# Gated delta net heads: key norms inside the last projection, and a chain that begins with the key and value transposes

## The chip, the cores and the metric

One Trainium2 chip, one core of it. The metric is the device time of one execution in microseconds (us): the median of several runs. Engines: TensorE (PE, with PEld for its weight loads), VectorE (DVE), ScalarE (ACT), GpSimd (POOL) and SyncE (SP), which issues DMAs.

## The reference

One layer of a hybrid decoder step in float32, for 2048 prompt tokens, 16 meta tokens ahead of them and 8 x 4 sample tokens; width 1024. Four retention heads and four gated delta net heads of 128 read one input projection; then come the output projection, a layer norm and a SwiGLU network, which the change does not touch. The part that matters, for one gated head in chunks of 128 tokens:

```python
gq = l2_norm(conv[..., :W]...) * (HEAD_DIM ** -0.5)
gk = l2_norm(conv[..., W:2 * W]...)
...
decay = exp(G_i - G_j), lower triangle;  kk = k @ k.T
lower = where(strict, kk * decay, 0.0) * beta[..., :, None]
sol = triangular_solve(eye(C) + lower, concat([v * beta, k * (beta * gam)]), unit_diagonal=True)
attn = (q @ k.T) * decay
def step(s, xs):
    u = wv - wk @ s
    o = qg @ s + at @ u
    s = cd * s + kt.T @ u
```

The q, k and v of the head go through a causal convolution of width 4 and silu first; beta is a sigmoid of the projection.

## The kernel before

The first half of the span is attention: four blocks of 512 tokens (the first also has a tile of 48 rows with the sample and meta tokens, its "side" chain). In a block the heads go in the order r0 g0 r1 g1 r2 g2 r3 g3 (r retention, g gated; the last block r0 g0 g1 r1 g2 g3 r2 r3). For each head `ret_proj` or `gdn_proj` issues the projection, dense matmuls of high and low parts (line L406), and the head's chain of small dependent steps (`ret_chain`, `gdn_chain` with `gdn_group`) is started when its projection is issued. So the front of head g0's chain is written between the projection matmuls of r1, and so on; the chains fill PE's stream, and PE's projection matmuls cover the chains.

How they mix is set in Python. A projection is a generator that yields the time of each matmul step. `advance(us)` counts that time down for each active chain, and lets a chain issue its next piece, up to its next `yield`, when its count is used up. Each `yield` of a chain names an entry of the table LAT, multiplied by a slack that `pace` works out as 0.9 x PROJ x (projections until the next gated head) / INVERSE: INVERSE is the sum of a gated chain's entries up to its scan, so that this part spreads over the projections at hand. The tile framework then turns the program order into priorities and sets each engine's order; what is quoted below is that compiled order. Each engine runs its own list in order.

A gated head, lines of the kernel before: `flip(0)` and `flip(1)` in `gdn_proj` transpose q and k into PSUM (tag pj, two buffers, which the projections use as well), take the sums of squares on ACT (L811), and copy the keys to SBUF as `kp` (L815). Behind the last projection come the inverse square roots (`rsqrt`, L266 to L278) and the factors gsk (L873, L874). `gdn_group` then makes, for four chunks at once, mg (L916), U1 matmuls (L919), the exponential E (L923, ACT), Es and E masked (L924, L925, POOL), scaled keys (L933, DVE), transposed values and vb (L936, L937), transposed keys and their copy kT (L941, L943), kk matmuls (L947), LT = kk * Es (L949, DVE), Z and U (L958, L959, DVE), and six masked copies of LT for the levels of the inverse, Lm (L961, POOL). The levels of the inverse follow (L965 to L1001), then the scan over the four chunks (L1020 to L1057), in which the state S (L1051, DVE) of one chunk is read by the next chunk's first matmul (L1033, L1034).

A retention head, lines shared by both kernels: each tile of 128 tokens is rotated by two DVE products out of PSUM (L569 into `qk`, L570 into `rotB`) and one POOL addition (L571). Its chain transposes qk (L628, PE) and scales the keys into `rkd` (L632, DVE). `rotB` has two buffers, `qk` five.

Layer norm of the next block is issued at fixed steps of r1, g1, r2 and g2 (LN_AT): L307 on DVE and two L309 on POOL per tile, among small steps.

Of the kernel before, what the change touches and what calls it, by code (L numbers as in the profile page):

```python
# [8 lines left out]
F32 = mybir.dt.float32  # L9
# [4 lines left out]
ALU = mybir.AluOpType  # L14
# [4 lines left out]
HD = 128  # L19
# [12 lines left out]
RMS_EPS = 1e-6  # L32
NBLK = 4
CPB = 4
LN_AT = [(x, i) for x in ("r1", "g1", "r2", "g2") for i in (18, 26)]
LAT = [1.0, 0.7, 0.7, 0.7, 2.0, 0.7, 0.5, 1.2, 1.8, 1.8, 1.0, 1.0, 1.7, 1.0, 0.6, 0.5, 0.5, 1.2]
PROJ = 25.0
INVERSE = 21.0
REST = 8.0
# [200 lines left out]
class Builder:  # L240
# [545 lines left out]
    def gdn_proj(self, b, h, G, out):  # L786
        nc, mp, cp = self.nc, self.mp, self.cvp
# [12 lines left out]
        kps = []  # L800

        def flip(a):

            for ts in sets:
# [7 lines left out]
                if a:  # L812
# [3 lines left out]
                    kps.append(kp)  # L816

        for piece in range(2):
            wh, wl = self.next_piece()
            for part in range(2):  # L820
# [9 lines left out]
                for (c0, n) in groups:  # L830
# [3 lines left out]
                    for i, us in enumerate(steps):  # L834
                        yield us
                        if i == 5 and which % 2 and c0 == groups[-1][0]:
                            flip(which // 2)
                    if which < 3:
# [9 lines left out]
                if which < 3:  # L848
# [21 lines left out]
                    cv.append(o)  # L870
        rn = self.rsqrt(sq.rearrange("p a b -> p (a b)"), 2 * nt, 128, self.sm, 1.0, 4.0 * RMS_EPS).rearrange("p (a b) -> p a b", a=2)
        sk = self.sm.tile([128, 2, nt], F32, tag="gsk", name="gsk")
        nc.vector.tensor_scalar(out=sk[:, 0], in0=rn[:, 0], scalar1=HD ** -0.5, scalar2=None, op0=ALU.mult)  # L873
        nc.vector.tensor_tensor(out=sk[:, 1], in0=rn[:, 1], in1=G["sb"][:, :, h], op=ALU.mult)  # L874
        out += [cv, zg, sk, kps]

# [19 lines left out]
    def gdn_group(self, b, h, cv, zg, sk, kp, G, mixd, ts, tiles):  # L896
# [16 lines left out]


        mg = big("mg")[:R, :, :R]
        nc.vector.tensor_tensor(out=mg, in0=bc(M1), in1=G["g"][:R, ts[0]:ts[0] + m, h].unsqueeze(2).broadcast_to([R, m, R]), op=ALU.mult)  # L916
        pe = wide()
        for i in range(m):
            nc.tensor.matmul(pe[:R, i, :R], lhsT=U1, rhs=mg[:, i, :], start=True, stop=True)  # L919
        yield LAT[6]  # L920
        E = big("E", 2)[:R, :, :R]
# [3 lines left out]
        nc.gpsimd.tensor_tensor(out=E, in0=E, in1=bc(M1), op=ALU.mult)  # L925


        kp = kp[:R]
        vb = big("vb", 2, n=128)[:R]
        lane = lambda a: a.unsqueeze(2).broadcast_to([R, m, 128])  # L930
        here = slice(ts[0], ts[0] + m)
        cq = sk[:R, 0, here]
        nc.vector.tensor_tensor(out=kp, in0=kp, in1=lane(sk[:R, 1, here]), op=ALU.mult)  # L933
        p = wide()[:R, :m, :]
        for i in range(m):
            nc.tensor.transpose(p[:, i, :], v[:, col(i):col(i) + R], self.ident)  # L936
        nc.vector.tensor_tensor(out=vb, in0=p, in1=lane(G["sv"][:R, here, h]), op=ALU.mult)  # L937
        yield LAT[7]
        pk = wide()
        for i in range(m):  # L940
            nc.tensor.transpose(pk[:, i, :R], kp[:, i, :], idn)  # L941
        kT = big("kT", 2)[:, :, :R]
        nc.scalar.copy(out=kT, in_=pk[:, 0:m, :R])  # L943
        yield LAT[8]
        pl = wide()
# [14 lines left out]
        for x in range(1, nl):  # L960
            nc.gpsimd.tensor_tensor(out=Lm[:, x - 1], in0=LT, in1=lvl(x), op=ALU.mult)  # L961
        yield LAT[9]
        pt = wide()[:R, :m, :R]
# [3 lines left out]
        for x in range(1, nl):  # L967
            yield LAT[10]
            py = wide()[:R, :m, :R]
# [3 lines left out]
            nc.vector.scalar_tensor_tensor(out=Z, in0=py, scalar=-1.0, in1=Ib, op0=ALU.mult, op1=ALU.add)  # L973
            yield LAT[11]
            pt = wide()[:R, :m, :R]
# [11 lines left out]
        nc.scalar.copy(out=V, in_=U)  # L987
        yield LAT[12]
        pe = wide()[:R, :m, :R]
# [5 lines left out]
        for it in range(2):  # L995
            yield LAT[13]
            pu = wide()[:R, :m, :R]
            for i in range(m):
                nc.tensor.matmul(pu[:, i, :], lhsT=Er[:, i, :], rhs=V[:, i, :], start=True, stop=True)
            V = big(f"V{it}", 1, F32 if it else F32R)[:R, :, :R]  # L1000
            nc.vector.tensor_tensor(out=V, in0=U, in1=pu, op=ALU.add)  # L1001
# [14 lines left out]
        for i in range(m):  # L1016
# [15 lines left out]
            else:  # L1032
                nc.tensor.matmul(pp[:, 0, :], lhsT=kT[:, i, :], rhs=S, start=True, stop=True)  # L1033
                nc.tensor.matmul(po[:, 1, :], lhsT=q[:, c0:c0 + R], rhs=S, start=True, stop=True)  # L1034
            yield LAT[14]
            nc.vector.scalar_tensor_tensor(out=r[:orow], in0=pp[:orow, 0, :], scalar=gc("ng", i, orow), in1=vb[:orow, i, :], op0=ALU.mult, op1=ALU.add)
# [5 lines left out]
            nc.scalar.copy(out=u, in_=pp[:R, 2, :])  # L1042
            yield LAT[15]
            if sp:
# [593 lines left out]
```

## Time and profile before

| | |
|---|---|
| median of 3 runs | 2992.69 us (2990.74 to 2993.83) |
| profiled execution | 2997.01 us, of which the span is 2995.2 us |
| mean granted TensorE clock | 0.982 |
| busy: PE, DVE, ACT, POOL | 96%, 65%, 33%, 26% |
| POOL, six Lm of all heads (L961) | 129.2 us |
| PE waiting for the scaled keys (L941 on L933) | 13.9 us, 7 times |

Rows of groups read: line, engine, operation, output<-inputs, partitions x elements and types, count, busy us, mean ns of one, and after the second bar the engine's idle time before them with what ended it. Rows of the timeline read: start, duration, then the same. A buffer's number is left out in the profile and stands behind its name in the orders below. The profile's times belong to the one profiled execution.

### The profile page before, as it was taken

To read this page: it belongs to the slowest core of one execution; us is meant where nothing else is said; L and a number is where in the kernel's file an instruction comes from. 1 tells how busy PE (TensorE), PEld (TensorE's weight loads), DVE (VectorE), ACT (ScalarE), POOL (GpSimd) and SP (SyncE) were. 2 spreads that over 40 slices of the span, in tenths; PEclk is the share of its full clock that TensorE was granted. 3 is DMA by queue.
4 is the path that set the end of the run, shared out by engine and by line. 5 is a ranking of instruction groups with operands and counts; after the bars stand their busy time and mean duration, and the time that the engine had idled before them with its cause. 6 is when DMAs were issued, how large, how long until landed. Compare 5 with 4: busy or idle time off the path is not lost.

```text
span 2995.2 us, 47489 instructions
## 1 busy us (share of the span) xinstructions
PE 2864.0 (96%) x17942; PEld 2554.5 (85%) x17942; DVE 1932.5 (65%) x4203; ACT 998.9 (33%) x2352; POOL 783.7 (26%) x761
## 2 busy tenths in 40 slices
PE   7999999999999999989988999999999999999997
PEld 6878888888888878877777999999999999988895
DVE  7777667766776676667766666667644444844456
ACT  2434334444444444433233333333211112321121
POOL 1312222221222122225543433433200101411111
PEclk8989999999999999999999999999999999999998
DMA  7544534444444333356658666667755555787762
GB/s 259 203 171 154 200 122 152 148 170 153 150 157 154 135 121 122 125 166 232 216 196 289 249 222 229 227 231 266 271 182 187 176 183 183 272 292 239 243 226 86
DMA packets 223093, 580.89 MB, mean 194 GB/s; under 512 B 27296, under 2 KB 62672, under 8 KB 206480
## 3 DMA queue, kind: packets, MB, share of 16 engines
q1 hardware_dynamic: 222864, 577.86, 55.5%
q8 instruction: 141, 2.31, 0.3%
q14 instruction: 88, 0.72, 0.1%
HBM read 409.48 MB, written 168.30 MB: 193 GB/s over the span
## 4 chain that ended last, share of the span: by engine, by line
PE 77%; DVE 13%; DMA 3%; ACT 3%; issue 3%; POOL 1%; SPq 1%; POOLq 0%; ACTq 0%; DVEq 0%
PE d L406 20%; PE pj L406 19%; PE Z L406 8%; PE X L406 8%; PE Y L406 8%; PE W L406 4%; ACT junk L811 1%; DVE cacc L860 1%; PE w L978 1%; PE w L971 1%; PE pj L712 1%; PE w L980 1%; PE rt L666 1%; DVE wl L356 1%; DMA fr<-gu 1%
## 5 line engine op out<-in xcount | busy, mean ns | idle before, releaser
L406 PE MATMUL pj<-wh,xT 128*128 128x256 f32 (+2 forms) x2176 | 460.6, 295 | 6.7 <-ACT wh L349 3.0
L406 PE MATMUL pj<-xT,wh 128*128 128x512 f32 (+1 forms) x1280 | 380.3, 381 | 1.8 <-ACT cpre L844 1.1
L406 PEld LDWEIGHTS pj<-wh,xT 128*128 128x128 f32 (+1 forms) x2176 | 354.5, 189 | 11.8 <-ACT wh L349 3.3
L1495 DVE TENSOR_TENSOR y<-y,d 128x512 f32<-128x512 f32 (+1 forms) x344 | 234.8, 683 | 172.6 <-PE d L406 172.4
L406 PE MATMUL pj<-wl,xT 128*128 128x256 f32 (+3 forms) x1088 | 311.1, 286 | 0.6 <-POOL wl L356 0.5
L406 PE MATMUL d<-dh,fh 128*128 128x512 f32 (+1 forms) x745 | 297.9, 400 | 13.5 <-ACT dh L349 7.0
L406 PE MATMUL d<-dh,fl 128*128 128x512 f32 (+1 forms) x745 | 295.3, 396 | 0.0
L406 PE MATMUL d<-dl,fh 128*128 128x512 f32 (+1 forms) x745 | 294.2, 395 | 0.5 <-DVE dl L356 0.5
L356 POOL TENSOR_TENSOR fl<-ta,fh 128x384 fp32r<-128x384 f32 (+1 forms) x65 | 63.2, 972 | 768.3 <-issue 542.4
L406 PEld LDWEIGHTS pj<-xT,wh 128*128 128x128 f32 x1280 | 212.3, 194 | 25.6 <-DVE S L714 3.4
L406 PE MATMUL pj<-xT,wl 128*128 128x512 f32 (+1 forms) x640 | 230.1, 360 | 0.0
L406 PEld LDWEIGHTS pj<-wl,xT 128*128 128x128 f32 (+1 forms) x1088 | 205.8, 189 | 1.4 <-POOL wl L356 0.8
L406 PEld LDWEIGHTS d<-dh,fl 128*128 128x128 f32 (+1 forms) x745 | 137.4, 184 | 38.8 <-issue 0.5
L406 PEld LDWEIGHTS d<-dh,fh 128*128 128x128 f32 (+1 forms) x745 | 137.5, 185 | 32.8 <-ACT dh L349 7.3
L406 PEld LDWEIGHTS d<-dl,fh 128*128 128x128 f32 (+1 forms) x745 | 137.5, 185 | 20.7 <-DVE dl L356 1.0
L406 PEld LDWEIGHTS pj<-xT,wl 128*128 128x128 f32 x640 | 122.9, 192 | 16.8 <-issue 0.8
L860 DVE SCALAR_TENSOR_TENSOR cacc<-cpre,cw,cacc 128x512 f32<-128x512 f32 (+1 forms) x144 | 115.8, 804 | 32.4 <-ACT cacc L858 30.9
L1394 DVE TENSOR_TENSOR u<-x,Y 128x384 f32<-128x384 f32 (+1 forms) x132 | 67.5, 511 | 100.7 <-PE Y L406 97.8
L961 POOL TENSOR_TENSOR Lm<-LT,lvl 128x512 f16<-128x512 f32 (+1 forms) x108 | 129.2, 1228 | 11.3 <-DVE LT L949 10.5
L349 ACT CAST fh<-ta 128x384 fp32r<-128x384 f32 (+1 forms) x66 | 31.8, 482 | 287.7 <-DVE ta L1402 287.7
L406 PE MATMUL X<-b,a11h 128*128 128x384 f32 (+1 forms) x528 | 125.5, 323 | 1.8 <-ACT a11h L349 1.8
L406 PE MATMUL X<-b,a12h 128*128 128x384 f32 (+1 forms) x528 | 126.1, 325 | 0.0
(389 smaller groups left out, 7164.1 us busy)
## 6 DMA issues: line engine op xcount, KB each, us to landing
wh<-parts SPq DMA_DIRECT2D x45, 1024.0 KB, 5.2
wl<-parts SPq DMA_DIRECT2D x45, 1024.0 KB, 6.7
fr<-dn SPq DMA_DIRECT2D x66, 512.0 KB, 5.4
fr<-gu SPq DMA_DIRECT2D x44, 512.0 KB, 4.7
s12h<-wd SPq DMA_DIRECT2D x44, 512.0 KB, 4.9
s12l<-wd SPq DMA_DIRECT2D x44, 512.0 KB, 5.6
s34h<-wd SPq DMA_DIRECT2D x44, 512.0 KB, 3.8
s34l<-wd SPq DMA_DIRECT2D x44, 512.0 KB, 4.8
```

The source lines that it names most:

```text
L349: i = nc.scalar.copy(out=h, in_=src)
L356: i = (nc.vector if el == "dve" else nc.gpsimd).tensor_tensor(out=l, in0=src, in1=h.bitcast(F32), op=ALU.subtract)
L406: self.nc.tensor.matmul(out, lhsT=a(k), rhs=b(k), start=first and k == 0 and i == 0, stop=last and k == kn - 1 and i == 2, skip_group_chec ...
L666: nc.tensor.matmul(po, lhsT=sc, rhs=v, start=True, stop=False)
L712: nc.tensor.matmul(p, lhsT=kt, rhs=ub[:, 4 * i:4 * i + 4, :].rearrange("p a e -> p (a e)"), start=True, stop=True)
L811: nc.scalar.activation(out=junk, in_=p[:, j, :], func=AF.Square, accum_out=sq[:, a, t:t + 1])
L860: nc.vector.scalar_tensor_tensor(out=ac, in0=pre[:, i:i + N], scalar=w(i), in1=ac, op0=ALU.mult, op1=ALU.add)
L961: nc.gpsimd.tensor_tensor(out=Lm[:, x - 1], in0=LT, in1=lvl(x), op=ALU.mult)
L971: nc.tensor.matmul(py[:, i, :], lhsT=Lm[:, x - 1, i, :], rhs=T[:, i, :], start=True, stop=True)
L978: nc.tensor.matmul(pt[:, i, :], lhsT=U[:, i, :], rhs=Z[:, i, :], start=True, stop=True)
L1394: add = lambda o, x, p: nc.vector.tensor_tensor(out=o, in0=x, in1=p, op=ALU.add)
L1495: nc.vector.tensor_tensor(out=ys, in0=ys, in1=p, op=ALU.add)
```

## The change

`norms()` now does the inverse square roots, the factors gsk and the scaling of `kp`, and it is called among the matmul steps of the last projection of the head (step 4 of its last group; in the first block step 1). The keys' transposes, sums of squares and copy, `flip(1)`, move ahead in that projection: from step 5 of its last group to step 1 of its first (in the first block step 3). The chain now begins with the transposes of keys (L931 after) and values (L943), goes on with the U1 matmuls (L948) and everything up to the six Lm (L970) in a second piece. Two yields of the chain are gone, and INVERSE goes from 21.0 to 19.4, the new sum. No instruction is added or taken away. The later entries of LAT keep their values under new numbers.

```diff
--- before.py
+++ after.py
@@ -33,9 +33,9 @@
 NBLK = 4
 CPB = 4
 LN_AT = [(x, i) for x in ("r1", "g1", "r2", "g2") for i in (18, 26)]
-LAT = [1.0, 0.7, 0.7, 0.7, 2.0, 0.7, 0.5, 1.2, 1.8, 1.8, 1.0, 1.0, 1.7, 1.0, 0.6, 0.5, 0.5, 1.2]
+LAT = [1.0, 0.7, 0.7, 0.7, 2.0, 0.7, 0.9, 2.8, 1.0, 1.0, 1.7, 1.0, 0.6, 0.5, 0.5, 1.2]
 PROJ = 25.0
-INVERSE = 21.0
+INVERSE = 19.4
 REST = 8.0
 LEVELS = (1, 2, 4, 8, 16, 32, 64)
 
@@ -815,6 +815,19 @@
                     nc.vector.tensor_copy(out=kp, in_=p[:, :m])
                     kps.append(kp)
 
+        def norms():
+
+            rn = self.rsqrt(sq.rearrange("p a b -> p (a b)"), 2 * nt, 128, self.sm, 1.0, 4.0 * RMS_EPS).rearrange("p (a b) -> p a b", a=2)
+            sk = self.sm.tile([128, 2, nt], F32, tag="gsk", name="gsk")
+            nc.vector.tensor_tensor(out=sk[:, 1], in0=rn[:, 1], in1=G["sb"][:, :, h], op=ALU.mult)
+            for kp, ts in zip(kps, sets):
+                r = tiles[ts[0]][0]
+                here = slice(ts[0], ts[0] + len(ts))
+                nc.vector.tensor_tensor(out=kp[:r], in0=kp[:r], in1=sk[:r, 1, here].unsqueeze(2).broadcast_to([r, len(ts), 128]), op=ALU.mult)
+            nc.vector.tensor_scalar(out=sk[:, 0], in0=rn[:, 0], scalar1=HD ** -0.5, scalar2=None, op0=ALU.mult)
+            sks.append(sk)
+
+        sks = []
         for piece in range(2):
             wh, wl = self.next_piece()
             for part in range(2):
@@ -833,8 +846,12 @@
                     steps = self.mm3g(p, lambda k: wh[:, k, o:o + 128], lambda k: wl[:, k, o:o + 128], lambda k: xh[:, k, c0:c0 + n], lambda k: xl[:, k, c0:c0 + n], 8, 1)
                     for i, us in enumerate(steps):
                         yield us
-                        if i == 5 and which % 2 and c0 == groups[-1][0]:
-                            flip(which // 2)
+                        if which == 1 and i == 5 and c0 == groups[-1][0]:
+                            flip(0)
+                        if which == 3 and c0 == 0 and i == (3 if b == 0 else 1):
+                            flip(1)
+                        if which == 3 and c0 == groups[-1][0] and i == (1 if b == 0 else 4):
+                            norms()
                     if which < 3:
                         if b == 0 and c0 == 0:
                             nc.scalar.copy(out=pre[:, :hs].rearrange("p (b t) -> p b t", t=7)[:, :, 3:7], in_=p[:, :NS].rearrange("p (b t) -> p b t", t=4))
@@ -868,11 +885,7 @@
                     else:
                         nc.vector.scalar_tensor_tensor(out=o[:, :T], in0=th, scalar=1.0, in1=ac, op0=ALU.add, op1=ALU.mult)
                     cv.append(o)
-        rn = self.rsqrt(sq.rearrange("p a b -> p (a b)"), 2 * nt, 128, self.sm, 1.0, 4.0 * RMS_EPS).rearrange("p (a b) -> p a b", a=2)
-        sk = self.sm.tile([128, 2, nt], F32, tag="gsk", name="gsk")
-        nc.vector.tensor_scalar(out=sk[:, 0], in0=rn[:, 0], scalar1=HD ** -0.5, scalar2=None, op0=ALU.mult)
-        nc.vector.tensor_tensor(out=sk[:, 1], in0=rn[:, 1], in1=G["sb"][:, :, h], op=ALU.mult)
-        out += [cv, zg, sk, kps]
+        out += [cv, zg, sks[0], kps]
 
     def gdn_chain(self, b, h, cvz, G, mixd):
 
@@ -912,36 +925,32 @@
         Ib, Ih, idn = bc(self.ident[:R, :R]), self.identh[:R, :R], self.ident[:R, :R]
 
 
+        kp = kp[:R]
+        pk = wide()
+        for i in range(m):
+            nc.tensor.transpose(pk[:, i, :R], kp[:, i, :], idn)
+        kT = big("kT", 2)[:, :, :R]
+        nc.scalar.copy(out=kT, in_=pk[:, 0:m, :R])
         mg = big("mg")[:R, :, :R]
         nc.vector.tensor_tensor(out=mg, in0=bc(M1), in1=G["g"][:R, ts[0]:ts[0] + m, h].unsqueeze(2).broadcast_to([R, m, R]), op=ALU.mult)
+
+        vb = big("vb", 2, n=128)[:R]
+        lane = lambda a: a.unsqueeze(2).broadcast_to([R, m, 128])
+        here = slice(ts[0], ts[0] + m)
+        cq = sk[:R, 0, here]
+        p = wide()[:R, :m, :]
+        for i in range(m):
+            nc.tensor.transpose(p[:, i, :], v[:, col(i):col(i) + R], self.ident)
+        nc.vector.tensor_tensor(out=vb, in0=p, in1=lane(G["sv"][:R, here, h]), op=ALU.mult)
+        yield LAT[6]
         pe = wide()
         for i in range(m):
             nc.tensor.matmul(pe[:R, i, :R], lhsT=U1, rhs=mg[:, i, :], start=True, stop=True)
-        yield LAT[6]
         E = big("E", 2)[:R, :, :R]
         Es = mg
         nc.scalar.activation(out=E, in_=pe[:R, 0:m, :R], func=AF.Exp)
         nc.gpsimd.tensor_tensor(out=Es, in0=E, in1=bc(ST), op=ALU.mult)
         nc.gpsimd.tensor_tensor(out=E, in0=E, in1=bc(M1), op=ALU.mult)
-
-
-        kp = kp[:R]
-        vb = big("vb", 2, n=128)[:R]
-        lane = lambda a: a.unsqueeze(2).broadcast_to([R, m, 128])
-        here = slice(ts[0], ts[0] + m)
-        cq = sk[:R, 0, here]
-        nc.vector.tensor_tensor(out=kp, in0=kp, in1=lane(sk[:R, 1, here]), op=ALU.mult)
-        p = wide()[:R, :m, :]
-        for i in range(m):
-            nc.tensor.transpose(p[:, i, :], v[:, col(i):col(i) + R], self.ident)
-        nc.vector.tensor_tensor(out=vb, in0=p, in1=lane(G["sv"][:R, here, h]), op=ALU.mult)
-        yield LAT[7]
-        pk = wide()
-        for i in range(m):
-            nc.tensor.transpose(pk[:, i, :R], kp[:, i, :], idn)
-        kT = big("kT", 2)[:, :, :R]
-        nc.scalar.copy(out=kT, in_=pk[:, 0:m, :R])
-        yield LAT[8]
         pl = wide()
         for i in range(m):
             nc.tensor.matmul(pl[:R, i, :R], lhsT=kT[:, i, :], rhs=kT[:, i, :], start=True, stop=True)
@@ -959,19 +968,19 @@
         for x in range(1, nl):
             nc.gpsimd.tensor_tensor(out=Lm[:, x - 1], in0=LT, in1=lvl(x), op=ALU.mult)
-        yield LAT[9]
+        yield LAT[7]
...
```

Line numbers from here on differ: LT is L958 after (L949 before), Lm L970 (L961), Z L967, U L968, r L1045, the state S L1060 (L1051), and the scan's first matmuls L1042 and L1043 (L1033, L1034).

What stands where on the engines, first on PE at the front of the chain of the second block's first gated head. `kp_7216` (before) and `kp_7179` (after) are its keys, `pj` rows the projection of the retention head that is issued meanwhile. Before:

```order
L1052 MATMUL w_7291<-u_7286,E_6386 128x128
L406 MATMUL pj_7340<-wh_7053,xT_5230 128x256
L406 MATMUL pj_7340<-wl_7054,xT_5230 128x256
L406 MATMUL pj_7340<-wh_7053,xT_5230 128x256 x2
L941 MATMUL w_7359<-ident_66,kp_7216 128x128 x4
L406 MATMUL pj_7340<-wl_7054,xT_5230 128x256
```

After:

```order
L406 MATMUL pj_7366<-wh_7053,xT_5236 128x256 x2
L406 MATMUL pj_7366<-wl_7054,xT_5236 128x256
L931 MATMUL w_7295<-ident_66,kp_7179 128x128 x4
L943 MATMUL w_7305<-ident_66,post_7140 128x128 x4
L948 MATMUL w_7333<-mg_7302,cb_271 128x128 x4
L956 MATMUL w_7342<-kT_7300 128x128 x4
L406 MATMUL pj_7366<-wh_7053,xT_5236 128x256 x2
```

The value transposes and the matmuls of mg, which stood some ten rows ahead of the key transposes, now stand behind them, and the kk matmuls directly after those.

On POOL at the same place; `qk_7336`, `qk_7388`, `qk_7441`, `qk_7486` are the four tiles of the retention head r1 (before), `qk_7362`, `qk_7407`, `qk_7441`, `qk_7492` the same four (after). Before:

```order
L309 TENSOR_TENSOR xa_7087<-xa_7087,xa_6604 128x512 x2
L924 TENSOR_TENSOR mg_7294<-E_7307,cb_271 128x512
L571 TENSOR_TENSOR qk_7336<-qk_7336,rotB_7335 128x256
L925 TENSOR_TENSOR E_7307<-E_7307,cb_271 128x512
L571 TENSOR_TENSOR qk_7388<-qk_7388,rotB_7387 128x256
L571 TENSOR_TENSOR qk_7441<-qk_7441,rotB_7440 128x256
L961 TENSOR_TENSOR Lm_7428<-LT_7426,lvl_273 128x512 x6
L571 TENSOR_TENSOR qk_7486<-qk_7486,rotB_7485 128x256
L309 TENSOR_TENSOR xa_7523<-xa_7523,xa_6604 128x512 x2
```

After:

```order
L309 TENSOR_TENSOR xa_7101<-xa_7101,xa_6611 128x512 x2
L571 TENSOR_TENSOR qk_7362<-qk_7362,rotB_7361 128x256
L952 TENSOR_TENSOR mg_7302<-E_7338,cb_271 128x512
L953 TENSOR_TENSOR E_7338<-E_7338,cb_271 128x512
L970 TENSOR_TENSOR Lm_7349<-LT_7347,lvl_273 128x512 x6
L571 TENSOR_TENSOR qk_7407<-qk_7407,rotB_7406 128x256
L571 TENSOR_TENSOR qk_7441<-qk_7441,rotB_7440 128x256
L571 TENSOR_TENSOR qk_7492<-qk_7492,rotB_7491 128x256
L309 TENSOR_TENSOR xa_7530<-xa_7530,xa_6611 128x512 x2
```

The additions of the second and third tile stood ahead of the six Lm, and now stand behind them.

On DVE at the same place, from the second tile's rotation on. Before:

```order
L569 TENSOR_TENSOR qk_7388<-pj_7340,rott_5247 128x256
L570 TENSOR_TENSOR rotB_7387<-pj_7340,rott_5247 128x256
L1036 SCALAR_TENSOR_TENSOR r_7378<-sc_7383,ng_5963,vb_6390 128x128
L632 TENSOR_SCALAR rkd_7776<-qk_7388,cb_271 128x128
L569 TENSOR_TENSOR qk_7441<-pj_7392,rott_5247 128x256
L570 TENSOR_TENSOR rotB_7440<-pj_7392,rott_5247 128x256
L949 TENSOR_TENSOR LT_7426<-w_7421,mg_7294 128x512
L958 TENSOR_TENSOR Z_7429<-LT_7426,lvl_273 128x512
L1051 SCALAR_TENSOR_TENSOR S_gdn0_298<-S_gdn0_298,eg_5957,sc_7383 128x128
L959 SCALAR_TENSOR_TENSOR U_7430<-Z_7429,ident_66 128x512
L1053 SCALAR_TENSOR_TENSOR O_7284<-qs_7381,eg_5957,w_7384 128x128
```

After:

```order
L944 TENSOR_TENSOR vb_7304<-w_7305,sv_5833 128x512
L958 TENSOR_TENSOR LT_7347<-w_7342,mg_7302 128x512
L569 TENSOR_TENSOR qk_7407<-pj_7366,rott_5253 128x256
L967 TENSOR_TENSOR Z_7350<-LT_7347,lvl_273 128x512
L570 TENSOR_TENSOR rotB_7406<-pj_7366,rott_5253 128x256
L968 SCALAR_TENSOR_TENSOR U_7351<-Z_7350,ident_66 128x512
L1045 SCALAR_TENSOR_TENSOR r_7397<-sc_7402,ng_5970,vb_6383 128x128
L632 TENSOR_SCALAR rkd_7776<-qk_7407,cb_271 128x128
L569 TENSOR_TENSOR qk_7441<-pj_7411,rott_5253 128x256
L570 TENSOR_TENSOR rotB_7440<-pj_7411,rott_5253 128x256
L1060 SCALAR_TENSOR_TENSOR S_gdn0_298<-S_gdn0_298,eg_5964,sc_7402 128x128
```

Of the second tile, L632 (`rkd`) stood ahead of LT, and now stands six rows behind it, followed by the third tile's rotation and by the state `S_gdn0`.

More of the change, by code (lines that the diff above doesn't have):

```diff
@@ L967, in gdn_group @@
         for x in range(1, nl):
-            yield LAT[10]
+            yield LAT[8]
             py = wide()[:R, :m, :R]
@@ L973, in gdn_group @@
             nc.vector.scalar_tensor_tensor(out=Z, in0=py, scalar=-1.0, in1=Ib, op0=ALU.mult, op1=ALU.add)
-            yield LAT[11]
+            yield LAT[9]
             pt = wide()[:R, :m, :R]
@@ L987, in gdn_group @@
         nc.scalar.copy(out=V, in_=U)
-        yield LAT[12]
+        yield LAT[10]
         pe = wide()[:R, :m, :R]
@@ L995, in gdn_group @@
         for it in range(2):
-            yield LAT[13]
+            yield LAT[11]
             pu = wide()[:R, :m, :R]
@@ L1034, in gdn_group @@
                 nc.tensor.matmul(po[:, 1, :], lhsT=q[:, c0:c0 + R], rhs=S, start=True, stop=True)
-            yield LAT[14]
+            yield LAT[12]
             nc.vector.scalar_tensor_tensor(out=r[:orow], in0=pp[:orow, 0, :], scalar=gc("ng", i, orow), in1=vb[:orow, i, :], op0=ALU.mult, op1=ALU.add)
@@ L1042, in gdn_group @@
             nc.scalar.copy(out=u, in_=pp[:R, 2, :])
-            yield LAT[15]
+            yield LAT[13]
             if sp:
@@ L1057, in gdn_group @@
             nc.scalar.activation(out=junk, in_=O[:orow, i, :], func=AF.Square, scale=cq[:orow, i:i + 1], accum_out=ss[:orow, i:i + 1])
-            yield LAT[16]
+            yield LAT[14]
         rs = self.rsqrt(ss[:orow], m, orow, self.sm, 1.0 / HD, RMS_EPS)
@@ L1062, in gdn_group @@
         nc.vector.tensor_tensor(out=O[:orow], in0=O[:orow], in1=rs.unsqueeze(2).broadcast_to([orow, m, 128]), op=ALU.mult)
-        yield LAT[17]
+        yield LAT[15]
         for i in range(m):
```

## Prediction

> **What bounds the kernel now.** I read the page first.
>
> ```profile
> span 2995.2 us, 47489 instructions
> PE 2864.0 (96%) x17942; PEld 2554.5 (85%) x17942; DVE 1932.5 (65%) x4203; ACT 998.9 (33%) x2352; POOL 783.7 (26%) x761
> PEclk8989999999999999999999999999999999999998
> ```
>
> TensorE is busy 96% of the span. A change that alters no instruction count can therefore only move the time in which PE waits, and the clock that it is granted. PE's waits by what ended them come second (total, times, longest, in us):
>
> ```profile
> PE w L941 <- DVE kp L933: 13.9, 7, 2.6
> PE w L919 <- DVE V L1001: 0.9, 4, 0.2
> PE pj L406 <- DVE kp L815: 0.7, 2, 0.4
> ```
>
> The key transposes L941 wait for the scaling of the keys, L933, and this is the largest wait at the front of a head's chain. The timeline of one such place, the second block's first gated head, shows why (start, duration, both in us):
>
> ```profile
> 568.69 1.28 POOL L924 TENSOR_TENSOR mg<-E,cb 128x512 f32<-128x512 f32 x1
> 568.94 1.05 DVE L277 SCALAR_TENSOR_TENSOR rqt<-rqt,rqa 128x8 f32<-128x8 f32 x1
> 571.09 1.26 POOL L925 TENSOR_TENSOR E<-E,cb 128x512 f32<-128x512 f32 x1
> 571.16 1.27 DVE L632 TENSOR_SCALAR rkd<-qk,cb 128x128 f32<-128x128 f32 x1
> 572.35 0.68 DVE L933 TENSOR_TENSOR kp<-kp,gsk 128x512 f32<-128x512 f32 x1
> 573.18 1.09 PE L941 MATMUL w<-ident,kp 128*128 128x128 f32 x4 [2.56 <-DVE kp L933]
> ```
>
> ```profile
> 934.96 1.09 PE L941 MATMUL w<-ident,kp 128*128 128x128 f32 x4 [2.57 <-DVE kp L933]
> ...
> 218.44 0.66 PE L941 MATMUL w<-ident,kp 128*128 128x128 f32 x4 [2.07 <-DVE kp L933]
> ```
>
> The first of these is the last of four alike (at 573, 646, 862 and 935 us); the other is the longest of the remaining three. DVE is late: its small steps of the norm wait in its queue, and L277 and L632 are drawn out to 1.05 and 1.27 us until the POOL multiplication beside them ends. Then come the windows around three such gaps (columns: the stretch, its length, PE, PEld, DVE, ACT, POOL busy, granted clock, DMA):
>
> ```profile
> 572.00:576.00 4.00, 2.82 (x14) 2.85 (x15) 1.75 (x5) 0.98 (x3) 0.35 (x1) 0.58 0.43 135
> 576.00:580.00 4.00, 4.00 (x36) 4.00 (x36) 1.70 (x6) 0.53 (x2) 0.73 (x1) 0.99 0.00 0
> ...
> 645.00:649.00 4.00, 2.69 (x19) 2.72 (x20) 2.90 (x8) 1.20 (x4) 0.72 (x2) 0.84 0.66 206
> 649.00:653.00 4.00, 4.00 (x28) 4.00 (x28) 0.31 (x2) 0.31 (x2) 0.49 (x1) 0.73 0.00 0
> 214.00:218.00 4.00, 2.12 (x16) 1.92 (x16) 3.95 (x15) 1.59 (x4) 0.72 (x1) 1.00 0.31 131
> 218.00:222.00 4.00, 3.56 (x29) 3.37 (x30) 3.87 (x10) 1.05 (x3) 0.74 (x1) 1.00 0.91 275
> ```
>
> A gap of 2.56 us costs more than itself: the clock behind it is 0.58 for 4 us, a loss of 0.42 x 4 = 1.7 us. At 645 to 653 it is (0.16 + 0.27) x 4 = 1.7 us. At 214 to 222, around the gap of 2.07 us, the clock stays 1.00. The row 576:580 also gives PE's pace at full clock: 36 records in 4.00 us, 0.111 us each.
>
> **What the change can gain.** The norms and the scaling move into the last projection, so that the transposes need not wait for them. At most this gains the 13.9 us, four clock losses of 1.7 us (6.8; the four of 2.56 or 2.57 us), and the small rows above (0.9 + 0.7): 22.3 us. It will not be all. In the four 2.5-us places the next block's layer norm runs on DVE and POOL at the same time, and the changed order on DVE still has the scaling (now L826) behind the elementwise step on E (0.68 in the row's form), L307 on 128x1024 (1.23), two small steps and one L570. Counted from the time at which E's matmuls were done before (566), E ends at 567 to 568, and the scaling at 569.7 to 570.8. PE has moved earlier too: 22 short matmuls (2.4 us) and two waits fewer stand before its transposes, which it reaches near 568.6 to 569.2. So about 0.5 to 2.2 us of wait stays in each of the four, with or without the 1.7 of clock: 2 to 16 us, and I take 8. The two waits fewer give the other steps 8% more spacing each, which I cost at nothing: PE has projection work between them. **Gain: 15 us, between 6 and 20.**
>
> **What the change can lose.** Here the order matters more than the edit. Before, POOL does the additions L571 of the following retention head's tiles between the chain's steps, and the six multiplications Lm come after the third. After, Es, E and the six Lm stand ahead of the second L571 (the orders are in the section on the change). And on DVE the reader of that second tile, L632 on qk_7407, moves to six rows behind LT. Each engine takes its instructions in order. So DVE has to wait at L632 until POOL has done Es, E, six Lm and one L571, all of which hang on this same chain. The durations (groups by form; the number before the bar is busy, then mean ns):
>
> ```profile
> L961 POOL TENSOR_TENSOR Lm<-LT,lvl 128x512 f16<-128x512 f32 x96 | 126.4, 1348 | 11.3 <-DVE LT L949 10.5
> L571 POOL TENSOR_TENSOR qk<-qk,rotB 128x256 f32<-128x256 f32 x64 | 48.3, 757 | 160.8 <-DVE rotB L570 141.6 <-DVE rqy L278 10.6 <-PE sc L1050 6.0
> L924 POOL TENSOR_TENSOR mg<-E,cb 128x512 f32<-128x512 f32 x16 | 20.7, 1296 | 113.4 <-ACT E L923 102.4 <-DVE rqt L276 11.0
> L925 POOL TENSOR_TENSOR E<-E,cb 128x512 f32<-128x512 f32 x16 | 20.4, 1272 | 0.6
> L923 ACT ACTIVATE E<-w 128x512 f32<-128x512 f32 x16 | 9.6, 597 | 16.0 <-PE w L919 16.0
> L569 DVE TENSOR_TENSOR qk<-pj,rott 128x256 f32<-128x256 f32 x64 | 26.7, 417 | 38.8 <-PE pj L406 38.6
> L959 DVE SCALAR_TENSOR_TENSOR U<-Z,ident 128x512 f16<-128x512 f16 x16 | 23.2, 1451 | 0.2
> L958 DVE TENSOR_TENSOR Z<-LT,lvl 128x512 f16<-128x512 f32 x16 | 11.7, 729 | 0.5
> L949 DVE TENSOR_TENSOR LT<-w,mg 128x512 f32<-128x512 f32 x16 | 11.0, 689 | 2.7 <-PE w L947 1.4
> L1051 DVE SCALAR_TENSOR_TENSOR S_gdn<-S_gdn,eg,sc 128x128 f32<-128x128 f32 x64 | 21.8, 341 | 22.3 <-PE sc L1050 22.0
> ```
>
> That such an addition really stands behind the six, and what they take together, is seen at 581 us of the timeline, where its operand from L570 was ready at 585.5 and it began at 589.0; there nothing on DVE needed it soon. The next row is what DVE waits for these additions now, in the whole run:
>
> ```profile
> 581.26 7.73 POOL L961 TENSOR_TENSOR Lm<-LT,lvl 128x512 f16<-128x512 f32 x6
> 585.10 0.41 DVE L570 TENSOR_TENSOR rotB<-pj,rott 128x256 f32<-128x256 f32 x1
> 588.96 0.77 POOL L571 TENSOR_TENSOR qk<-qk,rotB 128x256 f32<-128x256 f32 x1
> ...
> L961 POOL TENSOR_TENSOR Lm<-LT,lvl x108: 264/1164/1677, 119.3 to 1245.1; 128x512 f16<-128x512 f32 x96, 48x48 f16<-48x48 f32 x12
> ...
> DVE rkd L632 <- POOL qk L571: 10.6, 14, 2.0
> ```
>
> Take the head of the second block, and L as the end of the chain's first matmuls (L948 in the new code). Exp ends at L + 0.7, Es at L + 2.0, E at L + 3.3; the six Lm take 7.0 (six of the median 1.16) to 7.73, I take 7.4: L + 10.7. One L571: 11.4. L632, 0.28 undisturbed: 11.7. Behind it on DVE stand L569 and L570 of the third tile (0.8) and the state's update, 0.33: the state S is ready at L + 12.8. PE meanwhile: the kk matmuls (1 us), 29 short matmuls (3.2) and the load of the next one bring it near L + 4.6 to L1050, whose operand r stands on DVE behind LT, Z, two rotation steps and U: 2.0 + 0.7 + 0.4 + 0.7 + 0.4 + 1.4 + 0.35 = L + 5.95. It waits 1.4. Then 28 short matmuls, 3.1 us, and it stands at L1042 at L + 9.1, which reads S: it waits 3.7. Together 5.1 us, and the second wait is longer than the 2.56 that cost clock, so 1.7 on top: 6.8 us.
>
> This pattern, L632 six to twelve rows behind LT with its addition behind the six Lm, is in 14 of the 16 heads' orders; only two heads of the last block, followed by another gated head, are free of it. Counting the same rows in each: four heads as above, 4 x 6.8 = 27. Four heads where L632 is nine rows behind and PE's own rows last longer (waits 0.2 and 2.0, clock half the times, 0.8): 4 x 3.0 = 12. Two heads at a block's end, where the first tile's transposes L628 on PE and the splits of the next block's x also stand behind the addition (0.7 + 0.7 + 2.5 + 1.0, clock 1.7): 2 x 6.6 = 13. Four heads of the first block, where the small side chain's steps stand between: between the second and the first kind, 4 x 4.5 = 18. **Loss: 70 us.** Its lower end: if PE reaches S late, only the second kind everywhere, 14 x 2.2 = 31. Its upper end: 7.73 for Lm and 1.7 of clock for each of two waits, 14 x 7 = 98.
>
> **A rule beside it.** The pages bear on one term, the length of the six Lm. The Trainium skill ("SBUF — State Buffer", section "Who interferes with whom") says that DVE and GpSimd share one pair of ports as an exclusive lock, that a DVE instruction with two SBUF inputs contends with a GpSimd instruction reading SBUF, and that the loser blocks for the winner's whole instruction; the drawn-out L277 and, next to E, L632 agree. By it, a DVE that sits waiting leaves POOL alone, and the six would take the undisturbed 7.0 us rather than 7.4: the loss would be 14 x 0.4 = 6 us smaller, and the time 3042.
>
> **The sum.** +70 - 15 = +55 us against the profiled execution's 2997.0. That execution is 4.3 us above the median of the runs, 2992.7, and I set the sum on the median: 2993 + 55 = 3048 us.
>
> **Rivals.**
> First, the change does what it says and the additions cost nothing: faster. Place: L1042 in each head. It needs S by L + 9.1 instead of L + 12.8, so the six Lm would have to take 3.7 us in place of 7.4, 0.6 us each, or DVE's wait would have to fall where PE has other work of 4 us queued. The 1.16 of the median speaks against it. Time: 2993 - 15 = 2978, at best 2970.
> Second, the wait is there but smaller: PE is itself delayed by r and by its transposes, so that it comes to S later, and the clock stays up. The lower end, 31, less a gain of 15 to 20: 3004 to 3010. For it: gaps near 2 us cost no clock.
> Third, the wait is worse than summed: LT, which now follows Es closely, is late as well, and PE's short waits (0.2 to 1.4) add to the long one within one clock window. 98 - 10: 3080.
> Fourth, no change: gain and loss cancel, which takes a loss of 9 to 21 us, 1 us in each head.
>
> **How the numbers follow.** The summed case 0.62 (own range 3025 to 3068); smaller waits 0.16; worse waits 0.10; no net change 0.04; faster 0.08. A measurement of this kernel can hardly tell less than 0.2%, 6 us, from no change. Slower by more than that: 0.62 + 0.16 + 0.10 = 0.88; within it 0.04; faster 0.08. The range reaches from the second case's lower end to the third's value, 3003 to 3080; beyond it lie the faster case, no change, and a part of the worst.
>
> **What would show it.** In the changed kernel's waits, DVE L632 on POOL L571 should rise from 10.6 us, longest 2.0, to some 60 to 90 us, longest near 5 to 6. PE's waits on S at L1042, now absent among the large ones, should be the largest in attention, about 3.7 us each; the granted clock should show half-speed windows behind them. PE's wait for the keys' scaling should fall from 13.9 to about 5. If L632's wait stays near 10 us, the step on POOL's order is wrong, and the first rival holds. If PE waits at L1042 for under 1 us, DVE's wait lay beside other work. If Lm takes under 1 us each, its duration was the mistake.

## The result

The changed kernel takes 3048.0 us (median of 4 runs, 3046.1 to 3050.3); the kernel before took 2993.3 us beside it. The ratio is 1.0185, 95% interval 1.0173 to 1.0198: slower by 55 us. The forecast was 3048.

The profile's page of the changed kernel, and of its chain of waits the line by engine; behind them the same line of the kernel before:

```profile
span 3044.9 us, 47475 instructions
PE 2873.5 (94%) x17942; PEld 2567.2 (84%) x17942; DVE 1916.3 (63%) x4203; ACT 996.2 (33%) x2352; POOL 785.6 (26%) x761
PE 72%; DVE 11%; POOL 7%; issue 3%; DMA 3%; ACT 3%; SPq 1%; POOLq 0%; ACTq 0%; DVEq 0%
```

```profile
PE 77%; DVE 13%; DMA 3%; ACT 3%; issue 3%; POOL 1%; SPq 1%; POOLq 0%; ACTq 0%; DVEq 0%
```

No engine was given more work: each has as many instructions as before. POOL's busy time rose by 2 us, DVE's fell by 16, and PE's rose by 10, at a mean granted clock of 0.978 instead of 0.982. But POOL's part of the chain that ends last went from 1% to 7%. An engine that is busy a quarter of the time became one that others wait for. What PE waits for now (total, times, longest, in us), then the rows for r and S in the kernel before, and then the two rows of DVE that belong to it:

```profile
PE sc L1042 <- DVE S_gdn L1060: 20.6, 10, 3.5
...
PE sc L1050 <- DVE r L1045: 15.2, 13, 3.1
...
PE w L974 <- DVE U L968: 6.1, 3, 3.0
...
PE w L931 <- DVE kp L826: 3.2, 6, 0.7
```

```profile
PE sc L1041 <- DVE r L1036: 1.5, 1, 1.5
...
PE sc L1033 <- DVE S_gdn L1051: 0.6, 2, 0.3
```

```profile
DVE rkd L632 <- POOL qk L571: 55.4, 23, 5.9
...
DVE LT L958 <- POOL mg L952: 27.6, 12, 4.7
```

The change did what its words say: the key transposes' wait for the scaled keys fell from 13.9 to 3.2 us. Against that, DVE's wait for the additions rose from 10.6 to 55.4 us, and two waits of PE rose: on the state S, which DVE makes behind L632, from 0.6 to 20.6 us, and on r, which DVE makes ahead of L632 but now behind LT, Z and U, from 1.5 to 15.2 us. The place that the prediction worked through, in the timeline (start and duration in us; the brackets give the idle time before and what ended it):

```profile
584.83 1.27 POOL L952 TENSOR_TENSOR mg<-E,cb 128x512 f32<-128x512 f32 x1 [1.00 <-ACT E L951]
586.13 0.69 DVE L958 TENSOR_TENSOR LT<-w,mg 128x512 f32<-128x512 f32 x1 [1.38 <-POOL mg L952]
...
587.43 7.65 POOL L970 TENSOR_TENSOR Lm<-LT,lvl 128x512 f16<-128x512 f32 x6
...
589.90 0.49 PE L1050 MATMUL sc<-r,V 128*128 128x128 f32 x2 [1.51 <-DVE r L1045]
595.04 0.72 POOL L571 TENSOR_TENSOR qk<-qk,rotB 128x256 f32<-128x256 f32 x1
595.79 0.29 DVE L632 TENSOR_SCALAR rkd<-qk,cb 128x128 f32<-128x128 f32 x1 [5.95 <-POOL qk L571]
...
596.66 0.34 DVE L1060 SCALAR_TENSOR_TENSOR S_gdn<-S_gdn,eg,sc 128x128 f32<-128x128 f32 x1
...
597.05 0.69 PE L1042 MATMUL sc<-S_gdn,kT 128*128 128x128 f32 x2 [3.46 <-DVE S_gdn L1060]
```

The six Lm run from 587.4 to 595.0. The last operand of L571, from L570 on DVE, was ready at 588.4; L571 starts as the six end. DVE stands idle for 5.95 us at L632, with the state's update only three instructions behind it, and PE waits 1.51 us for r and 3.46 us for S. The windows around it (stretch, length, PE, PEld, DVE, ACT, POOL busy, granted clock, DMA):

```profile
590.00:594.00 4.00, 3.59 (x31) 3.34 (x31) 0.00 (x0) 0.27 (x1) 4.00 (x5) 1.00 0.00 0
594.00:598.00 4.00, 0.95 (x5) 0.95 (x6) 2.05 (x7) 0.65 (x3) 2.48 (x3) 0.90 0.00 0
598.00:602.00 4.00, 4.00 (x27) 3.99 (x27) 0.97 (x4) 0.75 (x3) 0.73 (x1) 0.67 0.39 111
```

In the first stretch DVE does nothing at all while POOL is busy throughout. The clock behind the wait is lowered for a while: (0.10 + 0.33) x 4 = 1.7 us more, the price that gaps of 2.56 us had before.

### The profile page after: what moved, and what is told of

It is laid out like the page before. It is cut to its first block, busy times and chain, and to the rows that moved or that the text cites. A ratio compares the mean times of both kernels' runs of the same rounds, so it can differ in the third digit from the quotient of the medians.

```text
span 3044.9 us, 47475 instructions
## 1 busy us (share of the span) xinstructions
PE 2873.5 (94%) x17942; PEld 2567.2 (84%) x17942; DVE 1916.3 (63%) x4203; ACT 996.2 (33%) x2352; POOL 785.6 (26%) x761
## 4 chain that ended last, share of the span: by engine, by line
PE 72%; DVE 11%; POOL 7%; issue 3%; DMA 3%; ACT 3%; SPq 1%; POOLq 0%; ACTq 0%; DVEq 0%
PE d L406 19%; PE pj L406 17%; PE X L406 8%; PE Y L406 8%; PE Z L406 8%; PE W L406 4%; POOL Lm L970 4%; DVE cacc L877 1%; POOL mg L952 1%; DVE rqt L272 1%; PE w L980 1%; PE pj L712 1%; PE w L987 1%; POOL E L953 1%; PE w L989 1%
## 5 line engine op out<-in xcount | busy, mean ns | idle before, releaser
L406 PEld LDWEIGHTS pj<-wh,xT 128*128 128x128 f32 (+1 forms) x2176 | 361.3, 193 | 13.8 <-ACT wh L349 4.2
L970 POOL TENSOR_TENSOR Lm<-LT,lvl 128x512 f16<-128x512 f32 (+1 forms) x108 | 130.4, 1238 | 0.2 <-DVE LT L958 0.2
L406 PE MATMUL W<-t,a22h 128*128 128x384 f32 (+1 forms) x528 | 126.3, 325 | 0.0
```

The costliest lines, as they stand in the source:

```text
L406: self.nc.tensor.matmul(out, lhsT=a(k), rhs=b(k), start=first and k == 0 and i == 0, stop=last and k == kn - 1 and i == 2, skip_group_chec ...
```

## The experiments

Theory 1: an addition L571 that DVE needs soon stands behind the six Lm in POOL's list; DVE waits in order, and PE with it. Theory 2: the front of the chain is too tight without its two yields, whatever POOL does. Theory 3: the norms and transposes cost, moved into the last projection. Each time is a median, each ratio against the kernel before in the same session.

**Half of Lm left out**, in the changed kernel (the later levels read the third copy again, so the inverse is not the true one and only the time counts):

```diff
-        for x in range(1, nl):
+        for x in range(1, min(nl, 4)):
             nc.gpsimd.tensor_tensor(out=Lm[:, x - 1], in0=LT, in1=lvl(x), op=ALU.mult)
...
-    nc.tensor.matmul(py[:, i, :], lhsT=Lm[:, x - 1, i, :], ...)
+    nc.tensor.matmul(py[:, i, :], lhsT=Lm[:, min(x, 3) - 1, i, :], ...)
```

> The changed kernel with three of the six masked copies Lm per head of four chunks left out (the higher levels of the inverse read the third copy, so the inverse is not the true one; this is read for its time alone). POOL's order is otherwise as in the changed kernel. Theory 1 (the additions L571 queued behind the six Lm on POOL hold L632 on DVE, and through it PE): the wait in each of the 14 heads shortens by three Lm, about 3.7 us, which takes it down to 1 to 2 us, and the clock losses with it: 3048 falls by 35 to 55 us, to 2993 to 3013. Theory 2 (the compressed front of the chain costs the time: two yields fewer, LT, Z and U late on DVE, whatever the additions do): POOL's six Lm are beside the path, the time stays within 3040 to 3050.

3006.5 us, ratio 1.004 (1.0025 to 1.0055): 42 us less than the changed kernel, as theory 1 has it. In its waits the row of PE for S at L1042 is gone; what is left are these two:

```profile
PE sc L1050 <- DVE r L1045: 15.1, 13, 3.1
...
DVE rkd L632 <- POOL qk L571: 24.1, 23, 2.6
```

PE's wait for r did not move by half of Lm. It has another cause, since r stands on DVE ahead of L632 and behind LT, Z and U. So theory 2 keeps a share.

DVE's wait at LT for Es fell as well, from 27.6 to 14.4 us. The changed kernel's rows by shape show where it was:

```profile
L958 DVE TENSOR_TENSOR LT<-w,mg 128x512 f32<-128x512 f32 x16 | 11.1, 692 | 14.1 <-POOL mg L952 11.6 <-PE sc L1059 2.4 <-PE w L956 0.2
...
L958 DVE TENSOR_TENSOR LT<-w,mg 48x48 f32<-48x48 f32 x4 | 0.8, 199 | 16.0 <-POOL mg L952 16.0
```

The four small LT belong to the side chain of the first block, whose Es stands on POOL behind the six Lm of the main chain. With half of Lm their 16.0 us fell to 2.8, while the 11.6 us of the others stayed. So POOL's order holds DVE in a second place too.

**The control**, the same cut in the kernel before:

> The kernel before with three of the six masked copies Lm left out in the same way as in the first experiment (read for its time alone). It is that experiment's control: if the 42 us that half of Lm gave in the changed kernel came from less work on POOL as such (less contention with DVE, earlier levels), this kernel gains much of it too, 20 to 40 us. Theory 1 (an addition that DVE needs soon stands behind Lm only after the change): within 5 us of the kernel before.

2984.9 us, ratio 0.9964 (0.9951 to 0.9977): 10 us faster, where theory 1 expected no more than 5. Less work on POOL is worth something in itself. If the two effects simply add, some 10 of the 42 us are of that kind, and about 32 belong to the queue. DVE's wait for the additions is the kernel before's, to the tenth: 10.6 us, 14 times, longest 2.0.

**The additions on DVE**, in the changed kernel:

```diff
-            nc.gpsimd.tensor_tensor(out=o, in0=o, in1=B[:, :, ::-1, :], op=ALU.add)
+            nc.vector.tensor_tensor(out=o, in0=o, in1=B[:, :, ::-1, :], op=ALU.add)
```

> The changed kernel with the addition L571 of the rotation done on DVE instead of POOL, everything else the same. It puts 68 additions (about 0.41 us each, 28 us in all) on DVE, and takes all L571 out of POOL's queue. Theory 1 (additions behind Lm): PE's waits on S at L1042 fall from 20.6 to under 4 us, and the time to 2998 to 3015, where the rest above the kernel before is LT waiting for Es and the extra DVE work. Theory 2 (compressed front): 3045 to 3060, since the front is as it was and DVE has more to do.

3034.5 us, ratio 1.0128 (1.0107 to 1.0150): 14 us less than the changed kernel, well short of the 2998 to 3015 that theory 1 gave. PE's wait for S fell from 20.6 to 2.3 us, as expected, but the time fell by less than half of what was expected. The same place of the timeline shows one reason; behind it stand the two rows of PE's waits:

```profile
588.77 8.04 POOL L970 TENSOR_TENSOR Lm<-LT,lvl 128x512 f16<-128x512 f32 x6
...
590.87 1.37 DVE L571 TENSOR_TENSOR qk<-qk,rotB 128x256 f32<-128x256 f32 x1
592.16 0.34 DVE L1045 SCALAR_TENSOR_TENSOR r<-sc,ng,vb 128x128 f32<-128x128 f32 x1
592.42 0.92 DVE L632 TENSOR_SCALAR rkd<-qk,cb 128x128 f32<-128x128 f32 x1
592.55 0.49 PE L1050 MATMUL sc<-r,V 128*128 128x128 f32 x2 [2.46 <-DVE r L1045]
...
PE sc L1050 <- DVE r L1045: 18.5, 13, 3.0
...
PE sc L1042 <- DVE S_gdn L1060: 2.3, 1, 2.3
```

The addition stands ahead of r on DVE now, and beside Lm it takes 1.37 us instead of the 0.41 I had put, which is right for the median (0.43). PE waits 2.46 us for r instead of 1.51, here and nearly the same in three more heads. Over the whole run PE's wait for S lost 18.3 us and its wait for r gained 3.3; the time fell by about the difference. Nothing of the clock came back: PE's busy time is 2873.6 us, the changed kernel's 2873.5, where half of Lm brought it down to 2859.1. My expectation was wrong in the price of the step and in the clock that would come back with it. So the experiment says that POOL's queue is not all, and cannot say how much it is.

**One yield back ahead of the kk matmuls**, with the sum of the waits unchanged, in two sizes:

```diff
-LAT = [..., 0.7, 0.9, 2.8, 1.0, 1.0, ...]
+LAT = [..., 0.7, 0.9, 1.8, 1.0, 1.0, ...]   # first kernel;  0.9, 1.0, 1.0, 1.0 in the second
+KKWAIT = 1.0                                # second: 1.8
...
+        yield KKWAIT
         pl = wide()
         for i in range(m):
             nc.tensor.matmul(pl[:R, i, :R], lhsT=kT[:, i, :], rhs=kT[:, i, :], start=True, stop=True)
```

> The changed kernel with one yield put back ahead of the kk matmuls, of 1.0 us, and the wait after Lm cut from 2.8 to 1.8, so that the sum of the waits (19.4) is the change's own. In its order the second tile's addition still stands behind all six Lm in 14 heads, with its reader six to twelve rows behind LT on DVE, as in the change. Theory 1 (POOL's queue): the loss mostly stays, 3020 to 3048; a part goes since LT no longer waits for Es. Theory 2 (the compressed front): with LT, Z and U a step later than Es the loss goes, 2980 to 3000.

> The same kernel as the one with 1.0 us, but with 1.8 us ahead of the kk matmuls and 1.0 after Lm: the same sum, one number moved by 0.8. In its order the second tile's addition is ahead of Lm again in all heads, and no reader of an addition behind Lm stands within 40 rows of LT on DVE. Theory 1: the stall is gone, 2975 to 2990. Theory 2: no different from the kernel with 1.0 us by more than some 10 us.

The first takes 3059.0 us, ratio 1.0214 (1.0198 to 1.0229); the second 2989.7 us, ratio 0.9982 (0.9973 to 0.9991). Moving 0.8 us from one wait to another, with the same instructions and the same sum of waits, is worth 69 us. What differs on POOL is this, in the second block's first gated head, the 1.0 kernel first, the 1.8 kernel second (lines are one or two higher than in the changed kernel; L572 is the addition):

```
L572 TENSOR_TENSOR qk_7343<-qk_7343,rotB_7342 128x256
L953 TENSOR_TENSOR mg_7302<-E_7338,cb_271 128x512
L954 TENSOR_TENSOR E_7338<-E_7338,cb_271 128x512
L972 TENSOR_TENSOR Lm_7379<-LT_7377,lvl_273 128x512 x6
L572 TENSOR_TENSOR qk_7407<-qk_7407,rotB_7406 128x256
```

```
L572 TENSOR_TENSOR qk_7343<-qk_7343,rotB_7342 128x256
L953 TENSOR_TENSOR mg_7302<-E_7338,cb_271 128x512
L954 TENSOR_TENSOR E_7338<-E_7338,cb_271 128x512
L572 TENSOR_TENSOR qk_7388<-qk_7388,rotB_7387 128x256
L972 TENSOR_TENSOR Lm_7412<-LT_7410,lvl_273 128x512 x6
```

The second tile's addition changes its place with the six Lm; the third tile's follows in both. The waits of the 1.0 kernel, then those of the 1.8 kernel:

```profile
PE sc L1044 <- DVE S_gdn L1062: 27.9, 9, 5.6
PE sc L1052 <- DVE r L1047: 16.1, 13, 4.9
...
DVE rkd L633 <- POOL qk L572: 73.5, 26, 6.0
```

```profile
PE w L976 <- DVE U L970: 8.9, 11, 1.9
...
PE sc L1052 <- DVE r L1047: 1.3, 5, 0.5
...
DVE rkd L633 <- POOL qk L572: 27.8, 26, 2.5
```

With the addition ahead of Lm PE's wait for S has no row any more, and the wait for r went with it, 16.1 to 1.3. Half of Lm had not moved the wait for r, and what changed for it here is DVE's order: in the 1.0 kernel r stands on DVE behind LT, Z and U, in the 1.8 kernel ahead of them (566.7 us, LT at 569.7). The edit moves LT, Z and U later as well as the addition, so the 69 us are those of the whole changed order and not of POOL's rows alone. Still it speaks against theory 2 as a tight front alone: the 1.0 kernel has the looser front of the two that share the bad order (LT waits 8.0 us for Es instead of 27.6), and it is the slowest of all. The front is not free either: the 1.8 kernel lies 12 us above the norms alone (below), and its wait for U is 8.9 us, against 1.3 there.

The 1.0 kernel was above the 3020 to 3048 expected, and its wait for S is 7 us longer than in the change. The reader stands six rows behind LT in eight of its heads, in the change in four. But 5.1 of the 7 us come from one head of the first block, where the wait for S went from 0.46 to 5.58 us, and there the cause is another. This step of DVE, ahead of the state's update, lasts 8.17 us beside POOL's Lm, where it takes 1.31 in the head worked through:

```profile
330.95 8.17 DVE L970 SCALAR_TENSOR_TENSOR U<-Z,ident 128x512 f16<-128x512 f16 x1
```

**Both yields back**, with the norms and the transposes as in the change:

> The changed kernel with two yields put back into the front of its chain (0.8 after the U1 matmuls, 1.8 ahead of the kk matmuls, 1.8 instead of 2.8 after Lm; INVERSE 21.0 again), the norms in the last projection and the transposes first as in the change. In its order on POOL the additions of the second and third tile stand ahead of the six Lm again, as before the change. Theory 1: the stall is gone and the gain of the moved norms remains: 2970 to 2985. Theory 2 (fewer yields cost): also under 2993. Theory 3 (the moved norms and the transposes at the chain's head are what costs, by putting their DVE and ACT work into the last projection): 3020 to 3050.

2983.9 us, ratio 0.9966 (0.9952 to 0.9979). **The norms alone**, in the chain of the kernel before (the line that scaled `kp` there is dropped, `norms()` and the new places of `flip(1)` are kept):

> The kernel before with only the norms moved: its chain keeps its order and its waits, without the scaling of the keys, which is now made in the last projection. Theory 1: the wait of L941 for the scaled keys (13.9 us and 6.8 us of clock) falls by half or more, and nothing is lost, since POOL's order is as before: 2973 to 2987. Theory 3 (the moved norms cost): 3000 to 3040.

2978.0 us, ratio 0.9942 (0.9925 to 0.9959); in a later session, again:

> The kernel with only the norms moved once more, as the measure for the two beside it: 2975 to 2980.

2982.2 us, ratio 0.9953 (0.9938 to 0.9968), 2 us above the range expected. Theory 3 falls: the norms are the change's gain, 13 to 16 us. The key transposes still wait a little, the first row for the norms alone, the second with both yields back and the transposes first:

```profile
PE w L953 <- DVE kp L826: 5.0, 5, 1.2
```

```profile
PE w L932 <- DVE kp L827: 7.3, 7, 1.6
```

**The chain alone**, with the norms where they were before (the scaling directly ahead of the key transposes):

> The chain of the change (transposes first, two yields fewer, sum 19.4) with the norms where they were: the inverse square roots and the scaling of the keys come at the chain's start. In its order an addition that DVE needs within 14 rows of LT stands behind the six Lm in 10 heads instead of 14. The four heads of the costliest kind (6.8 us each in the forecast) are free of it. The wait of the key transposes for the scaled keys is back at the chain's start. Theory 1: 3048 less 27 for the four heads, plus 16 for the norms' lost gain: 3030 to 3045. Theory 2 (compressed front): 3048 plus 16, 3058 to 3070.

3047.5 us, ratio 1.0175 (1.0153 to 1.0197): between the two forecasts, and so this one decides nothing by its time. PE's waits for S came out larger in fewer places, and the timeline of the first block shows that not all of them are the queue's:

```profile
PE sc L1030 <- DVE S_gdn L1048: 25.7, 6, 7.5
...
227.60 7.45 DVE L955 TENSOR_TENSOR Z<-LT,lvl 128x512 f16<-128x512 f32 x1
...
236.27 0.80 PE L1030 MATMUL sc<-S_gdn,kT 128*128 128x128 f32 x2 [7.43 <-DVE S_gdn L1048]
```

Four of the six waits, 2.5 to 2.8 us each, stand behind L632 and its addition. The other two, 7.43 and 7.46 us, lie in the first block, and there no addition that DVE needs soon stands behind Lm. Instead Z, which takes 0.73 us in the mean before the change, lasts 7.45 and 7.44 us beside the six Lm, and the state's update stands behind it on DVE. In a third head U lasts 7.79 us, and PE waits 5.96 us for it. So some 21 us of PE's waits here come from DVE steps drawn out beside POOL, which no theory had. A count of heads times a mean price does not carry over from one order to another.

**Beyond both.** The norms a matmul step earlier, and with two waits widened:

```diff
-LAT = [..., 1.0, 1.0, 1.7, 1.0, 0.6, 0.5, 0.5, 1.2]
+LAT = [..., 1.0, 1.2, 1.7, 1.0, 0.6, 0.5, 0.5, 1.9]
-INVERSE = 21.0
+INVERSE = 22.2
```

> Norms alone moved, one matmul step earlier: the keys' transposes at step 0 of the last projection and the norms at step 3 (first block: 3 and 0 of the last group). What is left of the wait for the scaled keys is 5.0 us in five places, longest 1.2. If DVE reaches the scaling a step (0.64 us) earlier, that falls to 2 to 3 us: 2974 to 2978. If the scaling waits behind other work on DVE in any case, nothing changes: 2977 to 2980.

> The same, with the wait ahead of the two products in each level 1.2 instead of 1.0 (sum 22.2 instead of 21.0) and the wait ahead of the output transposes 1.9 instead of 1.2. In the kernel with the norms alone moved PE waits 4.6 us at the products for Z and 4.5 us at the output transposes for O. If these waits are set by the spacing, 3 to 7 us go: 2969 to 2975; if by DVE's queue, or if the smaller spacing of the other steps opens waits there, 2975 to 2985.

2977.4 us (ratio 0.9943, 0.9924 to 0.9961) for the earlier norms, which is not told apart from the norms alone, though the wait for the scaled keys fell from 5.1 to 0.3 us; 2967.3 us (ratio 0.9902, 0.9885 to 0.9919) with the two waits, a little below the range expected: the fastest of these kernels, 28 us under the one before in the same session (2994.9). The two waits that were aimed at fell from 4.6 to 1.3 us (Z) and from 5.0 to 2.1 us (O).

## Why the prediction was right

**The gain, 15 us forecast.** The norms alone gave 13 and 16 us in two sessions. The wait left for the scaled keys was put at 0.5 to 2.2 us in four places; the row says 3.2 us in six, longest 0.7. It was less, and none of the six came near the 2.56 us behind which the clock had fallen.

**The loss, 70 us forecast.** The changed kernel is 66 to 70 us above the norms alone. Their profiled executions lie 68 us apart: PE stands idle 171.4 us of the span (3044.9 less 2873.5) against 122.4 (2977.1 less 2854.7), which is 49 us of waiting, and is busy 19 us longer with the same matmuls, at a granted clock of 0.978 against 0.984. The head worked through was forecast with waits of 1.4 us for r and 3.7 us for S, and measured 1.51 and 3.46, with 1.7 us of clock as put. By the step that it rested on, DVE's wait at L632 was to be 5 to 6 us at its longest and was 5.9; its total was put at 60 to 90 us and was 55.4.

**What was mis-sized or left out.** The four heads of the first kind came out as put, each with waits near 1.5 us for r and 3.46 for S and a lowered clock behind them, 27 us together. The four of the second kind were put too high: for S 1.10 to 1.38 us instead of 2.0, for r 0.52 instead of 0.2, and no lowered clock behind any, under 8 us instead of 12. Against that stand terms that were too small or missing. In the first block PE waits 2.96 and 3.10 us for r. The wait for U, 6.1 us in three places, was in no term; I had put only r's wait behind LT. And the small side chain's LT waits 16.0 us for its Es behind the main chain's Lm. This is POOL's order too, but at a place that the prediction did not look at; half of Lm took 13.2 us of it, and with it the longest of the waits for U (3.03 us).

Half of Lm left the wait for r where it was (15.1 of 15.2 us). It gave 42 us, some 10 of which it gives to the kernel before as well. So of the 70 us about 32, if the two effects add, hang on the length of Lm in the queue. The rest goes with the same change of order, as the 0.8 us moved between two waits and the kernel with both yields back show. How it divides between Lm's other half, the late LT and DVE's order ahead of r is open: the additions on DVE, meant to tell it, lengthened the wait for r and gave back no clock. That the sum came out to the microsecond is therefore partly luck between its terms.

**The rivals.** The one on the other side, the additions hidden, needed the six Lm in 3.7 us; they took 7.65. Smaller waits throughout would have shown S waits near 2 us everywhere: six of the ten lie between 0.46 and 1.38 us, and the four of 3.45 or 3.46, 13.8 of the 20.6 us, carried the case. The third rival had a part of the mechanism right, LT late behind Es and r behind it; its price, 3080, did not come.

**The rule beside the sum** gave 7.0 us for the six Lm where DVE waits, and 3042 us. The six took 7.65 at this place, and 1357 ns each over all (1348 before):

```profile
L970 POOL TENSOR_TENSOR Lm<-LT,lvl 128x512 f16<-128x512 f32 x96 | 127.3, 1357 | 0.2 <-DVE LT L958 0.2
...
L967 DVE TENSOR_TENSOR Z<-LT,lvl 128x512 f16<-128x512 f32 x16 | 18.8, 1176 | 0.3
```

The rule of the Trainium skill ("SBUF — State Buffer", section "Who interferes with whom") agrees with the trace here: Z, with two inputs in SBUF, runs beside POOL's E and the first Lm, and its mean went from 729 to 1176 ns. (L632, which the prediction named beside it, has one tensor as input and so does not bear on the rule for two.) What I worked out from it was wrong: DVE first does Z and U beside the first two Lm, which take 1.61 us each, and only then comes to its wait; the four behind them, with DVE idle, take 1.15 to 1.17.

## What to carry to other kernels

Moving or merging waits in a schedule written as generators changes the order on engines that the edit never names: compare each engine's order first, and look for an instruction that a busy engine needs soon and that now stands behind a long batch on an idle one. POOL was busy 26% of the time, and still some 30 us hung on half of the Lm in its list: an addition whose operands were ready at 588.4 us began at 595.0, when the six ahead of it had ended. Look also for steps of two engines that will run beside each other and did not before. A long batch of work whose results are needed one by one should not stand ahead of a short step that someone waits for.

## What the runs showed of the hardware

The granted clock does not go by the length of a single wait alone. Around 726 to 730 us of the changed kernel PE has three short waits, of 0.37, 0.69 and 0.54 us, and the clock behind them is lowered as after one of 2.56 us:

```profile
726.00:730.00 4.00, 2.68 (x17) 1.88 (x18) 4.00 (x10) 1.22 (x3) 0.00 (x0) 1.00 1.01 429
730.00:734.00 4.00, 4.00 (x22) 4.00 (x23) 3.21 (x6) 0.54 (x1) 0.00 (x0) 0.57 0.79 323
```

The single wait of 2.07 us in the kernel before, with PE busy 2.12 of 4.00 us around it, lowered nothing. With the additions on DVE, PE waits 2.46 us for r at 592.6 and at 666.5 us: behind the first the clock stays 1.00 up to 600, behind the second it is 0.72 from 668 to 672. The Trainium skill ("TensorE: Matmul & The Clock Gate", section "Why this matters for your kernels") advises against gaps over about 3 us; here a lowered clock followed waits well under that, and what decides among the shorter ones was not tested.

An addition that has a median of 0.43 us on DVE took 1.37 us beside POOL's multiplications, and a scaling next to it 0.92 where 0.28 is usual: moving a step off a queue may put it into contention with what stayed there.

A DVE step can also be held for far longer beside a run of POOL's. Z and U, which read two tensors in SBUF, lasted 7.45, 7.44, 7.79 and 8.17 us in four places of the first block (three in the kernel with the chain alone, one in that with 1.0 us ahead of kk). In each the six Lm ran on POOL meanwhile without a break, and the step ended 0.5 to 1.3 us after the sixth. In all other heads of these two kernels and of the changed one the same two steps took 0.7 to 1.7 us; what decides between the two was not tested.
